# A decoder trunk on one core: the order of all instructions computed in the kernel, instead of by the scheduler that the framework brings

## The chip, the cores and the metric

The kernel runs on 1 core of one Trainium2 chip. The metric is device time in microseconds (us). A core has five engines, each with an instruction queue of its own: TensorE (PE, matmuls and transposes), VectorE (DVE), ScalarE (ACT), GpSimd (POOL) and SyncE (SP, which here only issues transfers). POOL issues the transfers that accumulate into a tile in SBUF. Instructions of different engines are tied by semaphores.

## The reference, cut to what matters

One sequence of 512 tokens, width 1024, goes through two layers, a spatial-gating MLP and a retention, each followed by a dense feed-forward of 2816 hidden columns; all in float32.

```python
def reference(x, positions, mix_norm_g, ...):
    h = x
    for i in range(DEPTH):                       # DEPTH = 2
        hn = rmsnorm(h, mix_norm_g[i])
        if i % N_MIXERS == 0:
            h = h + sgu_mixer(hn, ...)           # gelu(hn @ w_in), u * (W_s LN(v) + b), @ w_out
        else:
            h = h + retention(hn, positions, ...)
        h = h + swiglu(rmsnorm(h, ffn_norm_g[i]), ...)   # (silu(a) * b) @ w_down
    return rmsnorm(h, final_norm_g)

def retention(h, positions, w_in, gn_g, w_out):  # 4 heads, chunks of 128 tokens
    q, k, v, g = jnp.split(h @ w_in, [...], axis=-1)
    q, k = rotary(q, positions), rotary(k, positions) * (RET_QK_DIM ** -0.5)
    scores = jnp.einsum('bhtd,bhsd->bhts', qc, kc) * decay_inner
    ...
    o = o * lax.rsqrt(jnp.mean(o * o, axis=-1, keepdims=True) + EPS)
    return (o.reshape(B, S, RET_V_WIDTH) * gn_g * jax.nn.silu(g)) @ w_out
```

## The kernel before

A float32 product is made of three matmuls on parts: `three` (L246 on) adds high x high, high x low and low x high; L247, L248 and L249 are these three. So each operand is split: ACT makes the high part (L216, `wh_...`), DVE the low part (L223, `wl_...`). The large products use a scheme of seven products in place of eight quarters (`seven`), with the sums of quarters in it named P1, P7, P6, Q4, P5, P2 and P3. A sum of weight blocks is made by DVE, or by an accumulating transfer that POOL issues into a tile already loaded (`add`, L349). A tile that carries P7, P6 and Q4 in turn is named `wr_..._P722`: after DVE has made the low part of one, the next block is added to it.

The residual X lies in SBUF, 4 chunks of 128 tokens by 1024. At a layer's end the last products come by chunk; `norm` sums squares on ACT (L636), `norm_factor` makes the factor (root on ACT L651, the rest on DVE), DVE scales to `xs_...` (L685), and `turn` (L663 on) transposes the chunk with 8 matmuls into a PSUM tile `xT_...`. From it ACT copies the high part `XH_...` (L671), DVE makes `XL_...` (L672), and in layers with `raw_copy` ACT copies it twice more, in halves, into `xr_...` (L704), from which the sums `xP7_...`, `xP5_...`, `xP6_...` of the next scheme are made. PSUM holds four such tiles of 1024 columns; a tile's slot is free when its last reader is done.

The first SGU product (`v0`) starts as chunks of x and weights come in. After the first feed-forward (units gu0_0 to gu0_5, down products dn0_0 and dn0_1) comes the retention: for head 0 the products qk0 and vg0, then rotation with the tables `CS` (sine and cosine, made by `rotary_tables` from positions in exact pieces: 41 DVE instructions of 128x512 in L854 to L895 and two Sin activations). A head ends with scores, values (`pv`), a norm, `sg`, and `turn_z` (L1239 on), which transposes into `zT` and copies to `z` (L1247); the output product `ro` takes the quarters of z and their sums `z_S` (L480) with high (L502) and low part (L506).

What sets the order: the code gives a list of jobs, one per step of matmuls, each with steps of preparation and a lead. `pipeline` runs a job's steps FETCH = 8 jobs ahead for a load, HIGH = 6 for the high part, PREP = 5 for the low part, ADD = 8 for accumulating transfers. Some transposes are put late by hand (`late_one`) or given `high_priority`; a few matmuls are tied behind others by `issue_after`. The rotary tables are cut in pieces by `yield`, and a piece is run after each product of the first feed-forward's unit 2 (`turn_tables`). Then the framework orders the program: the kernel is built with `tile.TileContext(nc, schedule_with_timeline_sim=True)`, which times the instructions on a model and orders each engine's queue by that; tiles are granted in the order in which the code asks for them, from 38 general tiles of 4 KB a partition (`N_GEN`), 5 of 2 KB (`N_TMP`) and the small pools.

Of the kernel before, what the change touches and what calls it, by code (L numbers as in the profile page):

```python
# [32 lines left out]
N_GEN = 38  # L33
N_TMP = 5
# [22 lines left out]
class Job:  # L57
# [3 lines left out]
    def __init__(self, run, steps=(), work=True):  # L61
        self.run, self.steps, self.work = run, list(steps), work


class Chain:
# [26 lines left out]
def pipeline(jobs):  # L92
    weighted = [j for j in jobs if j.steps]
    leads = sorted({n for j in weighted for n, _ in j.steps})
    at = dict.fromkeys(leads, 0)
    done = 0
    for job in jobs:
        for n in leads if done else leads[::-1]:
            while at[n] < min(len(weighted), done + n):
                for m, step in weighted[at[n]].steps:  # L100
                    if m == n:
                        step()
                at[n] += 1
        if job.steps:
            done += 1
        if job.work:
            Chain.all_step()
        job.run()


@with_exitstack
def trunk(ctx, tc, x, positions, mix_g, ffn_g, fin_g, sgu_w_in, sgu_w_s, sgu_b_s, sgu_ln_g, sgu_ln_b,
          sgu_w_out, ret_w_in, ret_gn_g, ret_w_out, ffn_w_gu, ffn_w_down, invf, decay, out):
    nc = tc.nc
    const = ctx.enter_context(tc.tile_pool(name="const", bufs=1))
    xpool = ctx.enter_context(tc.tile_pool(name="xpool", bufs=1))
    gen = ctx.enter_context(tc.tile_pool(name="gen", bufs=N_GEN))
    xp = ctx.enter_context(tc.tile_pool(name="xp", bufs=2))
    tmp = ctx.enter_context(tc.tile_pool(name="tmp", bufs=N_TMP))
    small = ctx.enter_context(tc.tile_pool(name="small", bufs=2))  # L120
    psp = ctx.enter_context(tc.tile_pool(name="psp", bufs=1, space=PSUM))

    W2 = 2 * T
    H = T // 2
# [34 lines left out]
    late = []  # L159
# [3 lines left out]
            late.pop(0)()  # L163

    ident = const.tile([P, P], F32, name="ident")
    make_identity(nc, ident)
# [662 lines left out]
    v = [[None, None] for _ in range(2)]  # L829
# [450 lines left out]
    t = [list(range(4 * hd, 4 * hd + 4)) for hd in range(HEADS)]  # L1280
# [39 lines left out]
```

## Time and profile before

| | us |
|---|---|
| median of 3 runs | 1202.37 (1201.17 to 1203.57) |
| the profiled execution, its own time | 1203.41 |
| its span, first to last instruction | 1201.7 |
| PE busy | 1180.0 |
| DVE busy | 960.9 |
| ACT busy | 664.6 |
| POOL busy | 171.0 |
| mean granted clock of PE | 0.996 |

Busy time is read per engine. A group's row gives line, engine, operation, output and inputs, shape, count, then busy time and mean length in ns, then the idle time of the engine just before, and what ended it. In a timeline row the first number is the start in us, the second the length, and square brackets hold the idle time ahead of it and its releaser. Names in the profile lack their numbers.

### The profile page before, as it was taken

The page shows a single profiled execution, that of the slowest core. Times are in us where ns is not written, and L with a number is a line of the kernel's source. Part 1 is how long each engine was busy: PE and PEld are TensorE (multiplying, and loading weights), DVE is VectorE, ACT ScalarE, POOL GpSimd, SP SyncE. Part 2 cuts the span into 40 slices and gives each one's busy share as a digit, 9 for nine tenths or more (in the row PEclk, how much of TensorE's full clock was granted, in tenths as well). Part 3 has the DMA queues.
Part 4 walks back from the last instruction along what each step waited for, and adds up shares of the span by engine and source line. Part 5 has one row for each costly group of instructions (what it writes and reads, how often), then busy time and mean ns, then how long its engine had stood idle before and what let it go on. Part 6 is the DMA issues. An engine that isn't in the chain of part 4 may idle for free.

```text
span 1201.7 us, 18455 instructions
## 1 busy us (share of the span) xinstructions
PE 1180.0 (98%) x7374; PEld 1067.4 (89%) x7374; DVE 960.9 (80%) x1143; ACT 664.6 (55%) x842; POOL 171.0 (14%) x151
## 2 busy tenths in 40 slices
PE   8999999999999999999999999999999999999997
PEld 7888899989999987988989898878899989999986
DVE  5587998899977789787885959879788896676897
ACT  5523775554444547555664656566565545535465
POOL 1000122121010130110201111220121210101210
PEclk9999999999999999999999999999999999999999
DMA  9912878898684898777677868877868887856892
GB/s 314 282 47 59 244 161 182 226 228 208 160 205 108 225 184 265 176 163 184 155 202 178 192 155 203 183 151 247 217 153 211 186 216 210 199 135 192 168 245 97
DMA packets 128167, 225.90 MB, mean 188 GB/s; under 512 B 7464, under 2 KB 30032, under 8 KB 128080
## 3 DMA queue, kind: packets, MB, share of 16 engines
q1 hardware_dynamic: 88848, 153.37, 38.6%
q0 software_dynamic: 38944, 70.81, 35.3%
q8 instruction: 58, 0.95, 0.3%
q10 hardware_dynamic: 288, 0.52, 0.1%
q14 instruction: 29, 0.24, 0.1%
HBM read 221.53 MB, written 2.10 MB: 186 GB/s over the span
## 4 chain that ended last, share of the span: by engine, by line
PE 85%; DMA 5%; issue 4%; DVE 2%; ACT 2%; POOL 1%; SPq 0%; DVEq 0%; POOLq 0%; ACTq 0%
PE X_gu L247 6%; PE X_gu L249 6%; PE X_gu L248 6%; DMA wr_gu_P<-in_ffn_w_gu 3%; PE Y_gu L249 3%; PE Y_gu L248 3%; PE Y_gu L247 3%; PE X_dn L247 3%; PE X_dn L248 3%; PE X_dn L249 3%; PE X_vg L247 2%; PE X_vg L248 2%; PE X_vg L249 2%; PE ps_v L247 1%; PE Y_dn L248 1%
## 5 line engine op out<-in xcount | busy, mean ns | idle before, releaser
L216 ACT ACTIVATE wh_gu_P<-wr_gu_P 128x1024 fp32r<-128x1024 f32 x132 | 135.3, 1053 | 87.6 <-DVE wr_gu_P L377 51.0
L223 DVE TENSOR_TENSOR wl_gu_P<-wr_gu_P,wh_gu_P 128x1024 fp32r<-128x1024 f32 x132 | 158.7, 1219 | 25.4 <-ACT wh_gu_P L216 25.1
L349 POOL DMA_DIRECT2D wr_gu_P<-in_ffn_w_gu x50 | 60.9, 1258 | 414.0 <-DVE wl_gu_P L223 196.2
L216 ACT ACTIVATE wh_dn_P<-wr_dn_P 128x1024 fp32r<-128x1024 f32 x72 | 69.1, 980 | 42.6 <-DMA wr_dn_P<-in_ffn_w_down 17.8
L223 DVE TENSOR_TENSOR wl_dn_P<-wr_dn_P,wh_dn_P 128x1024 fp32r<-128x1024 f32 x72 | 79.4, 1128 | 2.7 <-issue 1.1
L223 DVE TENSOR_TENSOR wl_vg_P<-wr_vg_P,wh_vg_P 128x1024 fp32r<-128x1024 f32 x48 | 57.8, 1217 | 14.5 <-ACT wh_vg_P L216 14.4
L349 POOL DMA_DIRECT2D wr_dn_P<-in_ffn_w_down x36 | 41.9, 1239 | 143.6 <-DVE wl_dn_P L223 46.6
L216 ACT ACTIVATE wh_vg_P<-wr_vg_P 128x1024 fp32r<-128x1024 f32 x48 | 49.2, 1055 | 22.8 <-DMA wr_vg_P<-in_ret_w_in 16.7
L349 POOL DMA_DIRECT2D wr_vg_P<-in_ret_w_in x26 | 31.5, 1248 | 207.5 <-DMA wr_vg_P<-in_ret_w_in 73.8
L247 PE MATMUL X_gu<-XH_f,wh_gu_P 128*128 128x256 f32 x176 | 50.6, 288 | 2.2 <-ACT xr_f L704 2.2
L247 PE MATMUL Z_gu<-XH_f,wh_gu_P 128*128 128x256 f32 x176 | 50.0, 284 | 1.4 <-DVE s L1051 1.4
L247 PE MATMUL X_gu<-xP5h_f,wh_gu_P 128*128 128x256 f32 x176 | 50.0, 284 | 0.9 <-ACT u L1026 0.9
L249 PE MATMUL Y_gu<-XH_f,wl_gu_Q 128*128 128x256 f32 x176 | 49.9, 284 | 0.8 <-DVE wl_gu_Q L223 0.8
L248 PE MATMUL X_gu<-XL_f,wh_gu_P 128*128 128x256 f32 x176 | 50.5, 287 | 0.0
L249 PE MATMUL X_gu<-XH_f,wl_gu_P 128*128 128x256 f32 x176 | 50.5, 287 | 0.0
L247 PE MATMUL X_gu<-xP6h_f,wh_gu_P 128*128 128x256 f32 x176 | 50.0, 284 | 0.2
L247 PE MATMUL Y_gu<-XH_f,wh_gu_Q 128*128 128x256 f32 x176 | 49.9, 284 | 0.0
L249 PE MATMUL Z_gu<-XH_f,wl_gu_P 128*128 128x256 f32 x176 | 49.9, 283 | 0.0
L248 PE MATMUL X_gu<-xP6l_f,wh_gu_P 128*128 128x256 f32 x176 | 49.8, 283 | 0.0
L249 PE MATMUL X_gu<-xP3h_f,wl_gu_P 128*128 128x256 f32 x176 | 49.8, 283 | 0.0
L248 PE MATMUL X_gu<-xP3l_f,wh_gu_P 128*128 128x256 f32 x176 | 49.8, 283 | 0.0
L249 PE MATMUL X_gu<-xP6h_f,wl_gu_P 128*128 128x256 f32 x176 | 49.8, 283 | 0.0
(643 smaller groups left out, 4284.5 us busy)
## 6 DMA issues: line engine op xcount, KB each, us to landing
wr_gu_P<-in_ffn_w_gu SPq DMA_DIRECT2D x110, 512.0 KB, 5.3
wr_gu_P<-in_ffn_w_gu POOLq DMA_DIRECT2D x50, 512.0 KB, 7.8
wr_dn_P<-in_ffn_w_down SPq DMA_DIRECT2D x50, 512.0 KB, 5.5
wr_vg_P<-in_ret_w_in SPq DMA_DIRECT2D x40, 512.0 KB, 5.8
wr_dn_P<-in_ffn_w_down POOLq DMA_DIRECT2D x30, 512.0 KB, 7.3
wr_vg_P<-in_ret_w_in POOLq DMA_DIRECT2D x26, 512.0 KB, 6.9
wr_ro_P<-in_ret_w_out SPq DMA_DIRECT2D x20, 512.0 KB, 4.8
wr_qk_P<-in_ret_w_in SPq DMA_DIRECT2D x15, 512.0 KB, 5.9
```

The source lines that it names most:

```text
L216: nc.scalar.activation(h, s, AF.Copy)
L223: nc.vector.tensor_tensor(l, s, f32(h), ALU.subtract)
L247: nc.tensor.matmul(o, ah, bh, start=start, stop=False, skip_group_check=True)
L248: nc.tensor.matmul(o, ah, bl, start=False, stop=False, skip_group_check=True)
L249: return nc.tensor.matmul(o, al, bh, start=False, stop=stop, skip_group_check=True)
L349: nc.gpsimd.dma_start(raw[p, 0, g, s][:, 0:nk, :], source(b, g, s, nk), accum_op=ALU.add)
```

## The change

Nothing of the computation, of its tiles' shapes or of the transfers changes. The engines and pools that `trunk` sees are replaced: `rec = Recorder(tc)`, and `nc, tc = rec, rec`. Each call on an engine is recorded as an `Op`, with the tiles and the parts of them that it reads and writes, and the earlier operations on which it depends. The calls to `pipeline` and the jobs now only set in which order operations are recorded; `issue_after` and `high_priority` do nothing. At the end `emit(rec)` computes an order and issues the calls in it, with the framework's own ordering switched off (`manual_schedule`). In the trace of the changed kernel every recorded instruction has the line of the call in `record` (L333).

The order is found in two passes. First, PE's operations in recorded order get the times at which they would run without any wait; `backward` walks from the end and gives each other operation the latest time (`late`) by which it must run for PE. Then a list simulation goes forward: PE takes the earliest recorded operation that can run, each other engine the one with the least `late` (plus three table loads if ACT would have to load another table). SBUF tiles are granted in order of `late`, so that a load is issued as soon as a tile is free for it; PSUM slots follow the recorded order.

```diff
+RESULT = 35
+TO_PE = 55
+HW_DMAS = 8
...
+    if name == "dma_start":
+        kind = "add" if "accum_op" in kwargs else "load" if writes else "store"
+        size = n * 4 * (writes or reads)[0].shape[0]
+        busy = {"SP": 450, "POOL": 1200, "ACT": 100}[engine]
+        took = busy
+        slow = max(60, size * (2 if kind == "add" else 1) * 1350 // 524288)
...
+LAND = 2200
+MARGIN = 600
+TABLE = 1290
...
+def order_of(rec, report=None):
...
+    for op in ops:
+        op.late = None
+        if op.engine == "PE":
+            op.late = at
+            at += op.busy
+    total = at
...
+    backward(ops, lazy, total, gap)
...
+    for key, tiles in classes.items():
+        tiles.sort(key=lambda t: min((o.late, o.n) for o in t.users))
...
+                if e == "PE":
+                    op = min((o for o in queue[e] if can(o)), key=lambda o: o.n, default=None)
+                else:
+                    for o in queue[e]:
+                        if can(o):
+                            if o.kind:
+                                fly = flying["sw" if e == "POOL" else "hw"]
+                                if len(fly) >= HW_DMAS and fly[-HW_DMAS] > now:
+                                    continue
+                            cost = o.late + (3 * TABLE if o.table and o.table != table else 0)
+                            if op is None or (cost, o.n) < best:
+                                op, best = o, (cost, o.n)
...
+    return sorted(ops, key=lambda o: (o.start, o.n))
+
+
+def emit(rec):
+    with rec.tc.manual_schedule():
+        for op in order_of(rec):
+            op.call()
...
-    nc = tc.nc
-    const = ctx.enter_context(tc.tile_pool(name="const", bufs=1))
...
+    rec = Recorder(tc)
+    nc, tc = rec, rec
...
     feed_forward(1, finish)
     pipeline(jobs)
+    emit(rec)
```

Three places of the two orders. In the rows, numbers behind a name are the part, group or step, the last one counts instructions.

At the retention's output, DVE's row before: `X<-X,Y_ro` adds a finished product to the residual, `z_S1_1` and `z_S2_1` are the sums for `z_P6`, of which PE needs the high and low part.

```order
L527 TENSOR_TENSOR X_95<-X_95,Y_ro_7684 128x2x512
L223 TENSOR_TENSOR wl_ro_P6_1_0_7700<-wr_ro_P722_1_0_7431,wh_ro_P6_1_0_7699 128x1024
L480 TENSOR_TENSOR z_S1_1_7749<-z2_1_7009,z3_1_7714 128x1024
L480 TENSOR_TENSOR z_S2_1_7751<-z_S1_1_7749,z2_0_7023 128x1024
L223 TENSOR_TENSOR wl_ro_P6_1_2_7745<-wr_ro_P722_1_2_7457,wh_ro_P6_1_2_7744 128x1024
L506 TENSOR_TENSOR z_P6l_1_7748<-z_S2_1_7751,z_P6h_1_7747 128x1024
```

And DVE's row there in the changed kernel:

```order
L333 TENSOR_TENSOR wl_ro_P6_1_2_7746<-wr_ro_P722_1_2_7502,wh_ro_P6_1_2_7719 128x1024
L333 TENSOR_TENSOR z_S1_1_7755<-z2_1_7039,z3_1_7734 128x1024
L333 TENSOR_TENSOR wl_ro_Q4_0_0_7765<-wr_ro_P722_0_0_7327,wh_ro_Q4_0_0_7751 128x1024
L333 TENSOR_TENSOR z_S2_1_7774<-z_S1_1_7755,z2_0_7069 128x1024
L333 TENSOR_TENSOR z_Q4l_0_7781<-z1_1_6365,z_Q4h_0_7761 128x1024
L333 TENSOR_TENSOR X_82<-X_82,Y_ro_7669 128x2x512
L333 TENSOR_TENSOR z_P6l_1_7802<-z_S2_1_7774,z_P6h_1_7789 128x1024
```

The two sums have moved from behind the residual's addition to ahead of it, and the weights of P6 and the first of Q4 stand ahead of both. On ACT, `z_P6h_1` now follows `wh_ro_Q4_0_0` and `wh_ro_Q4_0_2`, which it preceded; on PE the transposes `zT3_0` stand right behind `zT3_1` and not among the products of P6.

At the start of the second feed-forward, ACT's row before: `XH_f1` and `xr_f1` are copies of the transposed chunks `xT_f1_0` and `xT_f1_1`, `s1_1_0` a copy of a finished product.

```order
L671 ACTIVATE XH_f1_8143<-xT_f1_0_8370 128x8x128
L216 ACTIVATE wh_gu1_1_P1_0_2_8302<-wr_gu1_1_P111_0_2_8229 128x1024
L216 ACTIVATE wh_gu1_1_P2_0_0_8333<-wr_gu1_1_P221_0_0_8237 128x1024
L1026 ACTIVATE s1_1_0_8361<-X_gu1_0_8307 128x1024
L216 ACTIVATE wh_gu1_1_P2_0_2_8364<-wr_gu1_1_P221_0_2_8305 128x1024
L704 ACTIVATE xr_f1_0_0_8381<-xT_f1_0_8370 128x4x128
L671 ACTIVATE XH_f1_8143<-xT_f1_1_8446 128x8x128
L704 ACTIVATE xr_f1_0_1_8382<-xT_f1_0_8370 128x4x128
```

And in the changed kernel:

```order
L333 ACTIVATE XH_f1_8185<-xT_f1_0_8383 128x8x128
L333 ACTIVATE xr_f1_0_0_8408<-xT_f1_0_8383 128x4x128
L333 ACTIVATE xr_f1_0_1_8417<-xT_f1_0_8383 128x4x128
L333 ACTIVATE s1_1_0_8423<-X_gu1_0_8298 128x1024
L333 ACTIVATE wh_gu1_0_P6_0_2_8433<-wr_gu1_0_P722_0_2_8150 128x1024
```

All three readers of `xT_f1_0` now stand side by side.

The rotary tables on DVE, a piece of them before, in the first feed-forward's unit 2 (`s1_0_2`, `y7_0_2` are its gates):

```order
L869 TENSOR_TENSOR turns_2718<-sum11_2936,turn12_2938 128x512
L868 CAST turn14_3003<-turns13_3000 128x512
L1036 SCALAR_TENSOR_TENSOR s1_0_2_2678<-X_gu0_2_2611,s1_0_2_2678 128x512
L223 TENSOR_TENSOR wl_gu0_3_P6_0_0_3059<-wr_gu0_3_P722_0_0_2828,wh_gu0_3_P6_0_0_3058 128x1024
L1036 SCALAR_TENSOR_TENSOR y7_0_2_2749<-y7_0_2_2749,u2_0_2_2820 128x1024
L869 TENSOR_TENSOR frac13_3002<-turns13_3000,turn14_3003 128x512
```

And the last of them in the changed kernel, at the retention's start, where `xP7l_r` and `xP6l_r` are parts that vg0 needs and `ts_q0` is the first use of the tables `CS`:

```order
L333 SCALAR_TENSOR_TENSOR xP7l_r_5119<-xP7_r_5020,xP7h_r_5029 128x1024
L333 TENSOR_TENSOR sum17_5131<-turns_4891,frac16_5110 128x512
L333 TENSOR_TENSOR xP5_r_5138<-xr_r_0_0_4881,xr_r_0_1_4907 128x1024
L333 CAST turn18_5150<-sum17_5131 128x512
L333 TENSOR_TENSOR xP6_r_5154<-xP5_r_5138,xr_r_1_0_4737 128x1024
L333 TENSOR_TENSOR turns_4891<-sum17_5131,turn18_5150 128x512
L333 TENSOR_TENSOR wl_vg0_P6_0_0_5176<-wr_vg0_P722_0_0_4675,wh_vg0_P6_0_0_5069 128x1024
L333 TENSOR_SCALAR quarter_5189<-turns_4891 128x512
L333 TENSOR_TENSOR wl_vg0_P6_0_2_5195<-wr_vg0_P722_0_2_4706,wh_vg0_P6_0_2_5158 128x1024
L333 SCALAR_TENSOR_TENSOR xP6l_r_5202<-xP6_r_5154,xP6h_r_5183 128x1024
L333 CAST turn19_5212<-quarter_5189 128x512
L333 TENSOR_TENSOR ts_q0_5216<-ps_qk0_0_4793,CS_5193 128x1024
```

All 41 have moved from unit 2 to rows 428 to 500 of DVE, up to their first use in row 499. The load of `pos` stands 88 rows later in SP's queue. At the head of SP's queue, where x came first (two pieces of chunk 0, the first weight of v0, six pieces of the other chunks, then the other weights), pieces now alternate: the first weight of v0 and chunk 0 piece by piece, then a weight of v0 and a chunk in turn. ACT has 17 table loads instead of 14. At the tail ACT issues the output's first chunk ahead of the last sum of squares, and not behind it.

More of the change, by code (lines that the diff above doesn't have):

```diff
@@ L108, in pipeline, with __init__, view, __getitem__ @@
         job.run()
+ENGINE_OF = {"tensor": "PE", "vector": "DVE", "scalar": "ACT", "gpsimd": "POOL", "sync": "SP"}
+BANK = 512
+RESULT = 35
+TO_PE = 55
+HW_DMAS = 8
+class Virtual:
+    def __init__(self, rec, pool, shape, dtype, tag, name, bufs, psum):
+        import numpy as np
+        self.rec, self.pool, self.dims, self.dtype, self.tag, self.name, self.bufs = rec, pool, list(shape), dtype, tag, name, bufs
+        free = 1
+        for n in self.dims[1:]:
+            free *= n
+        self.grain = BANK if psum else max(1, free // 64)
+        self.index = np.broadcast_to(np.arange(free).reshape([1] + self.dims[1:]), self.dims)
+        self.users, self.left, self.real, self.history, self.granted = [], 0, None, [], None
+        self.first = None
+    def view(self):
+        return View(self, self.index, ())
+    def __getitem__(self, key):
+        return self.view()[key]
+    def __getattr__(self, name):
+        if name.startswith("_"):
+            raise AttributeError(name)
+        return getattr(View(self, self.index, ()), name)
+    def realize(self):
+        if self.real is None:
+            extra = {} if self.bufs is None else {"bufs": self.bufs}
+            if self.tag is not None:
+                extra["tag"] = self.tag
+            self.real = self.pool.real.tile(self.dims, self.dtype, name=self.name, **extra)
+        return self.real
@@ new lines, with __init__, shape, __getitem__ @@
+class View:
+    def __init__(self, tile, index, path):
+        self.tile, self.index, self.path = tile, index, path
+    @property
+    def shape(self):
+        return list(self.index.shape)
+    def __getitem__(self, key):
+        return View(self.tile, self.index[key], self.path + (("item", key),))
+    def rearrange(self, *a, **k):
+        return View(self.tile, self.index, self.path + (("rearrange", a, k),))
+    def bitcast(self, *a):
+        return View(self.tile, self.index, self.path + (("bitcast", a, {}),))
+    def to_broadcast(self, *a):
+        return View(self.tile, self.index, self.path + (("to_broadcast", a, {}),))
+    def realize(self):
+        t = self.tile.realize()
+        for step in self.path:
+            t = t[step[1]] if step[0] == "item" else getattr(t, step[0])(*step[1], **step[2])
+        return t
+    def mask(self):
+        import numpy as np
+        m = 0
+        for i in np.unique(self.index[0].ravel() // self.tile.grain):
+            m |= 1 << int(i)
+        return m
+    def width(self):
+        n = 1
+        for k in self.index.shape[1:]:
+            n *= k
+        return n
@@ new lines, with __init__, tile, pool @@
+class Pool:
+    def __init__(self, rec, real, bufs, psum):
+        self.rec, self.real, self.bufs, self.psum = rec, real, bufs, psum
+    def tile(self, shape, dtype, tag=None, name=None, bufs=None):
+        return Virtual(self.rec, self, shape, dtype, tag, name, bufs, self.psum)
+class Op:
+    __slots__ = ("n", "engine", "call", "before", "after", "tiles", "new", "busy", "took", "table", "kind", "start", "end",
+                 "late", "left", "ready", "ins", "what", "slow", "then")
+class Recorder:
+    def __init__(self, tc):
+        self.tc, self.real = tc, tc.nc
+        self.ops, self.held = [], {}
+        for attr in ENGINE_OF:
+            setattr(self, attr, EngineProxy(self, attr))
+    def pool(self, real, bufs, psum=False):
+        return Pool(self, real, bufs, psum)
+    def add(self, engine, call, reads, writes, what, busy, took, table=None, kind=None, slow=0):
+        op = Op()
+        op.n, op.engine, op.call, op.what, op.busy, op.took, op.table, op.kind = len(self.ops), engine, call, what, busy, took, table, kind
+        op.before, op.after, op.then, op.tiles, op.new, op.ins, op.slow = set(), [], [], [], [], None, slow
+        seen = set()
+        for views, w in ((reads, False), (writes, True)):
+            for v in views:
+                t, m = v.tile, v.mask()
+                for q, qm, qw in t.history:
+                    if q is not op and (w or qw) and qm & m:
+                        op.before.add(q)
+                if id(t) not in seen:
+                    seen.add(id(t))
+                    op.tiles.append(t)
+                    t.users.append(op)
+                    if t.first is None:
+                        t.first = op
+                        op.new.append(t)
+                        if t.pool.psum:
+                            was = self.held.get(t.tag)
+                            self.held[t.tag] = t
+                            op.before.update(was.users if was else ())
+        for views, w in ((reads, False), (writes, True)):
+            for v in views:
+                t, m = v.tile, v.mask()
+                if w:
+                    t.history = [h for h in t.history if h[1] & ~m]
+                t.history.append((op, m, w))
+        for q in op.before:
+            (q.then if q.engine == engine == "PE" else q.after).append(op)
+        self.ops.append(op)
+        return op
+    def issue_after(self, ins):
+        return nullcontext()
+    def high_priority(self):
+        return nullcontext()
@@ new lines, with backward, post, settle @@
+Recorder.record = record
+LAND = 2200
+MARGIN = 600
+TABLE = 1290
+def backward(ops, lazy, total, gap):
+    import heapq
+    events, serial = [], 0
+    free, pending = {}, {}
+    need, left = {}, {}
+    def post(back, op):
+        nonlocal serial
+        serial += 1
+        heapq.heappush(events, (back, serial, op))
+    def settle(op):
+        for q in op.before:
+            if q.engine != "PE":
+                need[q] = min(need.get(q, total), op.late - gap(op, q))
+                left[q] -= 1
+                if left[q] == 0:
+                    ready(q)
+    def ready(q):
+        place = "dma" if q.kind else q.engine
+        by = need.get(q, total) - (MARGIN if q.kind else q.took - q.busy)
+        pending.setdefault(place, []).append((q, total - by))
+        post(total - by, None)
+    for op in ops:
+        if op.engine != "PE":
+            left[op] = len(op.after)
+    for op in reversed(ops):
+        if op.engine == "PE":
+            post(total - op.late, op)
+        elif not op.after:
+            ready(op)
+    while events:
+        back, _, op = heapq.heappop(events)
+        if op is not None:
+            settle(op)
+        if events and events[0][0] == back:
+            continue
+        for place, queue in pending.items():
+            if free.get(place, back) > back:
+                continue
+            able = [q for q, at in queue if at <= back]
+            if not able:
+                continue
+            q = max(able, key=lambda o: (lazy[o], o.n))
+            queue[:] = [e for e in queue if e[0] is not q]
+            length = q.slow if q.kind else q.busy
+            free[place] = back + length
+            post(free[place], None)
+            q.late = total - back - length - (LAND + q.busy if q.kind else 0)
+            post(total - q.late, q)
```

182 lines of the change are left out of this document (175 added, 7 removed).

## Prediction

> **What bounds the kernel now.** First the busy times of the page, then the table of windows, to see where TensorE (PE) does not run.
>
> ```profile
> span 1201.7 us, 18455 instructions
> ## 1 busy us (share of the span) xinstructions
> PE 1180.0 (98%) x7374; PEld 1067.4 (89%) x7374; DVE 960.9 (80%) x1143; ACT 664.6 (55%) x842; POOL 171.0 (14%) x151
> ```
>
> PE is busy for 98% of the span, and the change takes no matmul away. So all that any other order can win is the time in which PE stands still or runs slowly. The windows say where that lies (columns: window, its length, then busy time of PE, PEld, DVE, ACT and POOL, the granted clock, DMA share, GB/s).
>
> ```profile
> 0.00:20.00 20.00, 16.47 (x71) 13.67 (x72) 10.72 (x16) 12.59 (x19) 3.12 (x12) 1.00 0.91 309
> 20.00:1180.00 1160.00, 1149.46 (x7244) 1042.49 (x7243) 936.49 (x1090) 641.89 (x805) 167.83 (x139) 1.00 0.75 188
> 1180.00:1201.70 21.70, 14.03 (x62) 11.27 (x61) 13.71 (x39) 10.15 (x21) 0.00 (x0) 0.92 0.26 98
> 480.00:500.00 20.00, 20.00 (x140) 18.69 (x139) 18.07 (x28) 13.25 (x23) 1.20 (x1) 1.00 0.74 207
> 500.00:520.00 20.00, 19.00 (x131) 17.23 (x130) 9.80 (x10) 10.59 (x13) 7.33 (x6) 1.00 0.79 139
> 800.00:820.00 20.00, 17.87 (x75) 14.04 (x74) 18.67 (x17) 12.45 (x15) 2.41 (x2) 0.91 0.90 234
> 860.00:880.00 20.00, 17.82 (x126) 16.94 (x125) 15.57 (x25) 12.52 (x18) 2.41 (x2) 0.93 0.60 124
> ```
>
> From 20 to 1180 us PE idles 1160.00 - 1149.46 = 10.5 us. Two windows also show a granted clock under 1: at half clock the share of slow time is twice what is missing, and half of that is lost, so 0.09 x 20 = 1.8 us and 0.07 x 20 = 1.4 us, 3.2 us in all. The middle of the kernel thus holds 13.7 us. The head (3.5 us idle) and the tail (7.7 us) are a matter of first loads and of the last norm. PE's waits, grouped by what ended them, name the causes:
>
> ```profile
> PE xT_in L667 <- DMA X<-in_x: 2.2, 1, 2.2
> PE X_gu L247 <- ACT xr_f L704: 2.2, 1, 2.2
> PE X_ro L247 <- ACT z_P6h L502: 1.6, 1, 1.6
> PE Z_gu L247 <- DVE s L1051: 1.4, 1, 1.4
> ```
>
> Apart from the first load, they are single waits of 1 to 2 us for ACT or DVE, which are busy for 55% and 80%: a matter of order more than of work.
>
> **Place A, the retention output (801 to 809 us).** DVE's timeline before PE's wait for z_P6h:
>
> ```profile
> 801.30 1.22 DVE L527 TENSOR_TENSOR X<-X,Y_ro 128x1024 f32<-128x1024 f32 x1 [2.90 <-PE Y_ro L249]
> 802.44 1.22 DVE L223 TENSOR_TENSOR wl_ro_P<-wr_ro_P,wh_ro_P 128x1024 fp32r<-128x1024 f32 x1
> 803.57 1.22 DVE L480 TENSOR_TENSOR z_S<-z,z 128x1024 f32<-128x1024 f32 x1
> 804.83 1.23 DVE L480 TENSOR_TENSOR z_S<-z_S,z 128x1024 f32<-128x1024 f32 x1
> ```
>
> DVE stood 2.90 us before X<-X,Y_ro until PE closed Y_ro, with the two z_S sums behind it in its queue. The changed order puts both sums ahead of that wait, and PE makes both zT tiles at the start of P7's second half. From there to the first X_ro matmul that needs z_P6, the second half of P7 (24 matmuls) and half of P6 (24) lie in program order. Two neighbours give the cadence:
>
> ```profile
> 800.19 0.39 PE L249 MATMUL Y_ro<-wh_ro_P,z_P7l 128*128 128x512 f32 x1
> 800.42 0.39 PE L247 MATMUL Y_ro<-wh_ro_P,z_P7h 128*128 128x512 f32 x1
> ```
>
> That is 0.23 us, 48 x 0.23 = 11.0 us. The chain is two ACT steps (copy of z, high part; 1.0 us each in ACT's rows of place B, the copy in four pieces somewhat more) and three of DVE (two sums, low part, 1.14 by the starts above): about 6 us, so 5 to spare. A new step stands on this path: z_P6h comes on ACT behind two wh_ro_Q4, whose tiles an accumulating transfer fills; it can eat the 5 us, not more than the rivals allow for below. I count A's 1.6 us as gone.
>
> **Place B, the second feed-forward's start (868 to 877 us).** ACT's timeline before the 2.2 us wait:
>
> ```profile
> 872.31 1.02 ACT L1026 ACTIVATE s<-X_gu 128x1024 f32<-128x1024 f32 x1
> 873.22 1.05 ACT L216 ACTIVATE wh_gu_P<-wr_gu_P 128x1024 fp32r<-128x1024 f32 x1
> 874.16 0.60 ACT L704 ACTIVATE xr_f<-xT_f 128x512 f32<-128x512 f32 x1
> 874.64 1.03 ACT L671 ACTIVATE XH_f<-xT_f 128x1024 fp32r<-128x1024 f32 x1
> 875.54 0.62 ACT L704 ACTIVATE xr_f<-xT_f 128x512 f32<-128x512 f32 x1
> ```
>
> X_gu of unit 1 needs the PSUM slot of xT_f1_0, which the second xr copy frees, at 876.16. By their starts, s and a weight copy (872.31 to 874.16) and the XH_f of the other chunk (874.64 to 875.54) were put before its two parts: 1.85 + 0.90 = 2.75 us, and two weight copies stand before the excerpt. In the changed order the two xr copies follow their XH_f directly, so the slot is free at least 2.75 us earlier and the 2.2 us go. What is late next there is the copies of chunk 1, which free their slot for a tile that comes later.
>
> At s (1.4) and the smaller places the rows of the changed order prepare weights earlier, or take the unit in program order. With the half clock after A and B, all 13.7 us may go. Whether the slow clock goes with the waits is a choice: the only two windows of the middle with a clock under 1 are those with A and B in them, so I take it that the waits bring it.
>
> The Trainium skill, page "TensorE: Matmul & The Clock Gate", section "What's actually happening", says that PE falls to half clock after an idle window of about 3.4 us. Here 1.6 and 2.2 us of waiting stood beside it, so the trace shows less than the page asks; by the page the slow spans would have some other cause, would stay, and the sum would be 3.2 us higher.
>
> **What the change adds.** Place E, the rotary tables: 41 DVE instructions, two Sin activations and the load of pos (88 rows later in SP's queue) leave the first feed-forward's unit 2 and come right before their use, at the retention's start. There DVE also makes XL_r, the xs_r, the sums of xr_r and the weights of vg0. Their durations, by groups:
>
> ```profile
> L869 DVE TENSOR_TENSOR frac<-turns,turn 128x512 f32<-128x512 f32 x5 | 3.4, 682 | 0.0
> ...
> L868 DVE CAST turn<-turns 128x512 int32<-128x512 f32 x5 | 2.2, 435 | 0.0
> ```
>
> In a filled queue each starts about 0.08 us before the one ahead ends (801.30 to 802.44 against 1.22), so I charge 1.14 for 128x1024, 0.60 for a sum of 128x512 and 0.35 for a cast or a scalar product; the 20 sums and 21 small ones of the tables are 12.0 + 7.4 = 19.4 us. From the last XL_r to the tc_q0 that frees ps_qk0 for Z_vg, the changed DVE row has 13 large, 12 middle and 12 small ones: 14.8 + 7.2 + 4.2 = 26.2 us. On PE the same stretch, from the last turn of xT_r (with its copy) to Z_vg, is 108 matmuls of qk0 with half the width (0.12 us each, an estimate from the 0.23) and 72 of vg0: 13 + 16.5, about 29 us. The low half of xP6 comes out at 21.8 against about 23.5 us. The rows ahead of that XL_r, from the last sums of X on, are 15.4 us by the same charges against 14 us of matmuls. So it fits with about a microsecond to spare or to lack: I take 1.0 us of new waits. The lower bound is nothing. The upper one comes from the windows: DVE has 1.9 + 10.2 = 12.1 us free from 480 to 520 us, but most of that is no free room, since it waits there for weights:
>
> ```profile
> 508.24 1.23 DVE L223 TENSOR_TENSOR wl_vg_P<-wr_vg_P,wh_vg_P 128x1024 fp32r<-128x1024 f32 x1 [4.42 <-ACT wh_vg_P L216]
> 513.92 2.36 DVE L223 TENSOR_TENSOR wl_vg_P<-wr_vg_P,wh_vg_P 128x1024 fp32r<-128x1024 f32 x2 [4.46 <-ACT wh_vg_P L216]
> ```
>
> If a fixed order has to sit those 8.9 us out too, 3.2 us are left for 19.4, and 16 us of waits come up. I lean on the row sums, because the changed row has done the weights of qk0 and half of vg0 before this stretch.
>
> Table loads: ACT loads 17 tables instead of 14. Two of the three lie where ACT waits anyway. The third (Sqrt) now stands between the last square and the first root of the norm after the spatial-gating output; before, that table was loaded earlier.
>
> ```profile
> 787.45 1.28 ACT L651 ACT_TABLE_LOAD   x1
> 788.75 0.29 ACT L651 ACTIVATE nf_o<-oss,eps 128x2 f32<-128x2 f32 x1
> ```
>
> That is 1.3 us more in the chain to the first turn of f0, which also stands after 5 matmuls of P3 and not after 12, 7 x 0.23 = 1.6 us earlier in PE's row. Before, PE did not wait for it, with a margin that no row gives: 1.0 us, between 0 and 2.9. The Trainium skill, page "ScalarE: Activation LUTs", section "What ACT_TABLE_LOAD costs", puts a switch at 2.66 us with its drain; the row above shows the next activation 1.30 us after the load began, and by the page this term would be 2.4.
>
> Accumulating transfers: as many as before and released by the same low parts; POOL issues them in almost the same order. Waits of under 1 us for them stay somewhere: 1.0, between 0 and 3.
>
> Head: SP's queue now alternates weights with X.
>
> ```profile
> 0.81 0.85 SPq L795 DMA_DIRECT2D X<-in_x  x2
> 1.72 0.91 SPq L809 DMA_DIRECT2D wr_v<-in_sgu_w_in  x2
> 2.67 3.02 SPq L795 DMA_DIRECT2D X<-in_x  x6
> ```
>
> Before, all of X but chunk 0 followed the first weights; now chunk 0 has two pieces of 256 KB ahead of or between its own and chunks 1 to 3 have one, two and three weights of 512 KB ahead of them. At 309 GB/s (first window) 512 KB are 1.7 us: chunk 0 and 1 come 1.7 us later, chunk 2 3.4, chunk 3 5.1, the weights as much earlier. PE needs both, and has 16 steps of 6 matmuls (1.36 us) to do; it starts later by up to 1.7 us and is fed evenly after that. I take +1.5 us; the bounds are -0.5 (earlier weights win) and +3 (the clock, slow until PE has run for a while, rises one span later).
>
> Tail: on ACT the two issues of the output's chunk 0 now stand ahead of the last square.
>
> ```profile
> 1194.90 0.38 ACTq L787 DMA_DIRECT2D out<-o  x1
> 1195.16 0.61 ACT L636 ACTIVATE sq_dn<-X 128x512 f32<-128x512 f32 x1
> 1195.32 0.46 ACTq L787 DMA_DIRECT2D out<-o  x1
> ```
>
> They cost up to 0.38 + 0.46 us, less what the earlier norms of chunks 2 and 3 win: +0.3, between -0.5 and +1.
>
> **The sum.** The profiled execution took 1203.41 us (span 1201.7 and 1.7 around it), 1.04 above the median of the runs, 1202.37. So 1203.41 - 13.7 + (1.0 + 1.0 + 1.0) + 1.5 + 0.3 = 1194.5, and at the median's scale 1193.5 us. Its own range: with none of the additions, the head at -0.5 and the tail at 0, 1188.2; with E and transfers at 3 and the head at its 3, 1200.0 (2.0 + 2.0 + 1.5 and 1.0 of the rest over the forecast).
>
> **The rivals.**
> *The waits only move* (chance 0.13): a fixed order can stand behind a transfer that lands late, as z_P6h may behind wh_ro_Q4; for it speaks that each queue runs in order. With as much new waiting as old (10.5), but no slow clock, 1203.4 - 13.7 + 10.5 + 1.8 - 1.0 = 1201.0: no measurable change.
> *The slow clock is not brought by these waits* (0.09): then 3.2 us stay, 1196.7. Against it: of the windows of the middle only those two are slow. The Trainium skill's page on TensorE, as told above, speaks for it.
> *The rotary tables fill DVE at the retention's start* (0.10), which ends slower: 16 us of waits there in place of 1.0, and PE then falls to half clock once (1.6, the mean of the two windows): 1193.5 + 15.0 + 1.6 = 1210.1. It decides once all new waits pass 14 us, 13.7 - 1.8 + 2.4. For it speaks that DVE and its wait for weights leave 3.2 us for 19.4, against it the sum of the rows.
> *The order is in effect the old one* (0.02): 1202.4. Against it speak the rows: the tables, the z sums and the xr copies have moved as shown.
>
> **How the numbers follow.** A measurement of this kernel tells about 0.2% from no change, 2.4 us: below 1200.0 is faster, above 1204.8 slower. The forecast has 0.66. Faster: 0.66, 0.09 of the clock rival and 0.02 of the moving waits, 0.77. Same: 0.11 of the moving waits and 0.02 of the last, 0.13. Slower: 0.10. The range goes from 1187 (the lower end, 1188.2, less a microsecond of delays that the windows count as busy, since ends of matmuls are modelled) to 1203, which holds the moving waits and leaves out the rotary rival.
>
> **What would show it.** Idle of PE from 20 to 1180 us near 3 us rather than 10.5; no window there with a clock under 1; no wait of PE for z_P6h or for xr_f before unit 1; Z_vg and xP6 waiting under 2 us in all; a wait of about 1 us at xT_f0; the first ps_v matmul at 10 to 11.5 us. The forecast is wrong if PE's waits name weights or transfers at new places with 10 us together, or if the time from 480 to 520 us holds several us of PE waiting for DVE.

## The result, and the profile after

The changed kernel takes 1265.01 us (median of four runs, 1261.81 to 1267.90) against 1201.77: 1.0523 times as long, with a 95% interval of 1.0495 to 1.0551. The forecast was 1193.5 us, and slower had been given one chance in ten. The profiled execution took 1265.18 us, its span is 61.7 us longer than before. One run of a variant below (both numbers changed) took 1659 us at a granted clock of 0.656 and is left out of the ratios; all others had 0.986 or more. First the busy times of the page:

```profile
span 1263.4 us, 18478 instructions
## 1 busy us (share of the span) xinstructions
PE 1195.9 (95%) x7374; PEld 1071.5 (85%) x7374; DVE 964.8 (76%) x1143; ACT 676.1 (54%) x845; POOL 170.6 (14%) x151
```

The instructions are the same but for the three table loads. ACT is busy 11.5 us longer, of which the loads (1.28 us each) are 3.8 and the rest stays open; PE is busy 15.9 us longer, which is taken apart below. The table of windows, cut at the head and the tail as before:

```profile
0.00:20.00 20.00, 15.60 (x65) 12.80 (x66) 10.19 (x15) 14.16 (x22) 3.13 (x12) 1.00 0.91 329
20.00:1240.00 1220.00, 1166.40 (x7252) 1047.84 (x7251) 941.03 (x1090) 652.67 (x804) 167.50 (x139) 0.99 0.72 178
1240.00:1263.40 23.40, 13.91 (x61) 10.85 (x59) 13.54 (x40) 9.26 (x21) 0.00 (x0) 0.93 0.24 91
```

In the middle PE now idles 1220.00 - 1166.40 = 53.6 us where it idled 10.5. That is 43.1 of the 61.7 us. PE's waits say for whom, and how often (columns: in total, times, longest):

```profile
PE X_gu L333 <- DVE s L333: 10.9, 8, 3.4
PE X_gu L333 <- ACT s L333: 5.5, 2, 3.2
PE pv L333 <- ACT osq L333: 4.8, 6, 0.8
PE sc L333 <- DVE s L333: 3.6, 3, 2.1
PE X_ro L333 <- DVE X L333: 3.4, 2, 2.7
PE ps_u L333 <- DVE ur L333: 3.1, 4, 0.8
PE X_dn L333 <- DVE X L333: 2.8, 2, 2.0
PE ps_v L333 <- ACT v L333: 2.4, 3, 0.8
```

The waits of before (z_P6h, xr_f ahead of a unit, s ahead of Z_gu) are not in the list. In their place stand many short ones, most near 0.8 us, and nearly all of one kind. One of them in PE's timeline, and DVE's at the same time:

```profile
251.07 0.28 PE L333 MATMUL X_gu<-xP3h_f,wl_gu_P 128*128 128x256 f32 x1
251.19 0.28 PE L333 MATMUL X_gu<-xP3h_f,wh_gu_P 128*128 128x256 f32 x1
251.31 0.28 PE L333 MATMUL X_gu<-xP3l_f,wh_gu_P 128*128 128x256 f32 x1
252.37 0.39 PE L333 MATMUL X_gu<-xP3h_f,wl_gu_P 128*128 128x256 f32 x1 [0.78 <-DVE s L333]
252.59 0.28 PE L333 MATMUL X_gu<-xP3h_f,wh_gu_P 128*128 128x256 f32 x1
```

```profile
251.62 0.69 DVE L333 SCALAR_TENSOR_TENSOR s<-X_gu,s 128x512 f32<-128x512 f32 x1 [1.89 <-PE X_gu L333]
252.23 1.22 DVE L333 SCALAR_TENSOR_TENSOR y<-y,u 128x1024 f32<-128x1024 f32 x1
```

The matmul at 251.07 is the last on the first half of the PSUM tile X_gu; the next two already write the second. DVE takes the first half, for the gate's product `s`. It could have begun when the first half was done (251.07 + 0.28 = 251.35), but it begins at 251.62, right behind the end of the second of the other two (251.31 + 0.28 = 251.59; ends of matmuls are modelled). PE stops in the midst of the second half and goes on when DVE is done, though it needs nothing that DVE makes there: its low part wl_gu_P is DVE's work too, but DVE had stood idle for 1.89 us before `s`. PE starts 1.06 us after the matmul before it, where 0.12 is usual: a wait of 0.78 costs 0.94.

Over PE's whole timeline (waits over 0.25 us, after the first 20 us) 43 waits of 43.7 us have matmuls on the same PSUM tile, by its name, on both sides, and 42 of these end with an instruction that reads this tile; 6 of 10.6 us lie between two tiles. Before, there were 6 of each kind, with 5.3 and 5.0 us, and only 1 of the 6 within a tile ended with a reader of it: the other 5 were for an operand. The clock records of the trace show half clock for 23.9 us ahead of the tail, before for 6.8 (the last stretch, at the span's end, is 5.6 us and was 5.7).

So the 61.7 us are 43.1 of idle time in the middle, 1.7 by which the window of the tail is longer, and 1166.40 - 1149.46 = 16.9 of more busy time in the middle. Of these 16.9, the slow clock is (23.9 - 6.8) / 2 = 8.5, the interruptions about 5.9 (37 more waits at the 0.16 of the one above, an estimate), and work that the head left over 16.47 - 15.60 = 0.9; 1.6 stay open.

### The profile page after: what moved, and what is told of

Same layout as the page of the kernel before. It is cut to its first block, busy times and chain, and to the rows that moved or that the text cites. A ratio compares the mean times of both kernels' runs of the same rounds, so it can differ in the third digit from the quotient of the medians.

```text
span 1263.4 us, 18478 instructions
## 1 busy us (share of the span) xinstructions
PE 1195.9 (95%) x7374; PEld 1071.5 (85%) x7374; DVE 964.8 (76%) x1143; ACT 676.1 (54%) x845; POOL 170.6 (14%) x151
## 5 line engine op out<-in xcount | busy, mean ns | idle before, releaser
L333 DVE TENSOR_TENSOR wl_gu_P<-wr_gu_P,wh_gu_P 128x1024 fp32r<-128x1024 f32 x132 | 158.7, 1220 | 54.2 <-ACT wh_gu_P L333 34.9
L333 ACT ACTIVATE wh_gu_P<-wr_gu_P 128x1024 fp32r<-128x1024 f32 x132 | 135.8, 1054 | 103.5 <-DMA wr_gu_P<-in_ffn_w_gu 44.1
L333 POOL DMA_DIRECT2D wr_gu_P<-in_ffn_w_gu x50 | 60.9, 1272 | 399.1 <-DVE wl_gu_P L333 170.5
L333 ACT ACTIVATE wh_dn_P<-wr_dn_P 128x1024 fp32r<-128x1024 f32 (+1 forms) x72 | 69.5, 983 | 66.4 <-PE X_gu L333 25.0
L333 DVE TENSOR_TENSOR wl_dn_P<-wr_dn_P,wh_dn_P 128x1024 fp32r<-128x1024 f32 (+1 forms) x72 | 80.5, 1131 | 15.2 <-PE X_gu L333 5.3
L333 POOL DMA_DIRECT2D wr_dn_P<-in_ffn_w_down x36 | 41.8, 1208 | 185.4 <-DMA wr_dn_P<-in_ffn_w_down 93.9
L333 DVE TENSOR_TENSOR wl_vg_P<-wr_vg_P,wh_vg_P 128x1024 fp32r<-128x1024 f32 x48 | 57.5, 1219 | 9.0 <-ACT wh_vg_P L333 7.9
L333 POOL DMA_DIRECT2D wr_vg_P<-in_ret_w_in x26 | 31.6, 1243 | 203.2 <-DVE wl_vg_P L333 71.4
L333 PE MATMUL X_gu<-xP3l_f,wh_gu_P 128*128 128x256 f32 x176 | 51.4, 292 | 7.0 <-DVE s L333 7.0
L333 ACT ACTIVATE wh_vg_P<-wr_vg_P 128x1024 fp32r<-128x1024 f32 x48 | 48.8, 1060 | 16.5 <-DMA wr_vg_P<-in_ret_w_in 11.6
L333 PE MATMUL X_gu<-xP6h_f,wh_gu_P 128*128 128x256 f32 x176 | 51.5, 292 | 5.5 <-ACT s L333 5.5
L333 PE MATMUL X_gu<-xP3h_f,wl_gu_P 128*128 128x256 f32 x176 | 51.8, 294 | 4.7 <-DVE s L333 3.9
L333 PE MATMUL X_gu<-xP3h_f,wh_gu_P 128*128 128x256 f32 x176 | 51.1, 290 | 0.8 <-DVE he L333 0.8
L333 PE MATMUL X_gu<-xP5h_f,wh_gu_P 128*128 128x256 f32 x176 | 49.9, 284 | 1.7 <-ACT u L333 1.7
L333 PE MATMUL X_gu<-xP6l_f,wh_gu_P 128*128 128x256 f32 x176 | 51.0, 290 | 0.0
L333 PE MATMUL X_gu<-xP6h_f,wl_gu_P 128*128 128x256 f32 x176 | 51.0, 290 | 0.0
L333 PE MATMUL Y_gu<-xP7h_f,wh_gu_P 128*128 128x256 f32 x176 | 50.5, 287 | 0.0
L333 PE MATMUL Y_gu<-xP7l_f,wh_gu_P 128*128 128x256 f32 x176 | 50.4, 286 | 0.0
L333 PE MATMUL Y_gu<-xP7h_f,wl_gu_P 128*128 128x256 f32 x176 | 50.3, 286 | 0.0
L333 PE MATMUL X_gu<-XH_f,wh_gu_P 128*128 128x256 f32 x176 | 50.0, 284 | 0.0
L333 PE MATMUL Z_gu<-XH_f,wh_gu_P 128*128 128x256 f32 x176 | 49.9, 284 | 0.0
L333 PE MATMUL Z_gu<-XL_f,wh_gu_P 128*128 128x256 f32 x176 | 49.9, 284 | 0.0
```

Of the source, the lines that this page charges most:

```text
L333: return fn(*[real_of(a) for a in args], **{k: real_of(a) for k, a in kwargs.items()})
```

## Experiments

Theory 1: an instruction that touches one half of a PSUM tile waits for those issued ahead of it, on other engines, that touch the other half. The planner keeps the halves apart (BANK = 512 elements, a tile has 1024) and so plans no wait. Theory 2: DVE and ACT run late behind transfers, wherever the halves stand. What theory 1 asks of PE's order can be read from the two orders with their waits. Before, at the end of unit 2 (rows shortened to the places where the tile changes):

```
X_gu0_2 <- xP3h_f0, wl_gu0_2_P3_0_2       last matmul of the first half
X_gu0_3 <- XH_f0, wh_gu0_3_P1_0_0         48 matmuls of the next unit's P1, and one of its P7
X_gu0_2 <- xP3h_f0, wh_gu0_2_P3_0_0       first matmul of the second half [waits DVE]
```

In the old order 49 other matmuls stand in front of the wait on DVE. In the changed order the second half follows the first directly.

**The planner told of whole tiles.** One number:

```diff
-BANK = 512
+BANK = 1024
```

> One number of the planner is changed: parts of a PSUM tile are told apart by 1024 elements (the whole tile) and not by 512 (its halves). Theory 1 (an instruction that touches one half of a PSUM tile waits for all issued ahead of it on other engines that touch the other half; the planner does not know it): the 43 waits of 43.7 us in which the matmuls before and after write the same PSUM tile go nearly all, and with five of them the half clock behind them, about 8 us; 1265 - 52 = 1213 us, 1205 to 1222. Theory 2 (ACT and DVE run late behind transfers, wherever the halves stand): waits stay at the same places, 1255 to 1270 us.

Measured 1225.79 us, 1.0198 times before (1.0182 to 1.0214). The waits within a tile fall from 43 to 4, from 43.7 to 3.5 us, and only one of the four ends with a reader of the tile: theory 1 holds, and theory 2 alone is out. But the time is 4 us over theory 1's range and 13 us over what I expected, since the waits between tiles grew from 10.6 to 20.2 us, and half clock is still 23.9 us. The largest of them:

```profile
PE X_gu L333 <- ACT s L333: 6.0, 2, 3.4
PE xT_f L333 <- DVE xs_f L333: 4.1, 3, 2.2
PE X_gu L333 <- ACT u L333: 3.8, 1, 3.8
```

ACT's timeline ahead of the first of the two waits for s (2.6 us, PE goes on at 295.6):

```profile
287.84 1.04 ACT L333 ACTIVATE wh_gu_P<-wr_gu_P 128x1024 fp32r<-128x1024 f32 x1
293.59 1.06 ACT L333 ACTIVATE wh_gu_Q<-wr_gu_P 128x1024 fp32r<-128x1024 f32 x1 [4.71 <-DMA wr_gu_P<-in_ffn_w_gu]
294.55 1.00 ACT L333 ACTIVATE s<-X_gu 128x1024 f32<-128x1024 f32 x1
```

The copy s, which frees X_gu for P6, stands behind a weight whose accumulating transfer was issued at 283.62 and landed at 293.50, 9.9 us later. By its constants the planner counts 1.2 + 2.2 + 2.7 = 6.1 us for it if no other transfer is ahead, where the median of POOL's 50 transfers into wr_gu is 7.7 us in this run (7.8 before), and 4.0 for a load, where the median of the 110 into wr_gu is 5.1. That is theory 3: a second cause.

**The same order, readers issued later.** The computed order stays, but each ACT or DVE instruction on a PSUM tile goes behind the matmuls on it that followed, up to the first instruction that needs its result:

```diff
+def readers_later(ops):
+    at = {op: i for i, op in enumerate(ops)}
...
+            end = min([at[q] for q in op.after + op.then], default=len(ops))
...
+            late = [at[q] for t in op.tiles if t.pool.psum for q in t.users if q.engine == "PE" and i < at[q] < end]
+            if late:
+                place[op] = (max(late), 1, i)
...
-        for op in order_of(rec):
+        for op in readers_later(order_of(rec)):
```

> The order is that of the changed kernel, but each ACT or DVE instruction that uses a PSUM tile is issued behind the matmuls on that tile that stood next behind it, as far as nothing that needs it comes. Theory 1 (order of issue makes the wait): PE no longer waits between the halves, the readers come one to three us later; the same-tile waits fall from 43.7 us to under 10, other waits grow by some us; 1215 to 1235 us. Theory 2 (late queues): nothing is won, since the readers come later still; 1262 to 1275 us.

Measured 1241.81 us, 1.0328 (1.0300 to 1.0356): 23 us won by making readers later. The waits within a tile halve only, to 21 of 21.0 us, where I expected under 10 (I take it that the limit often comes before the half's end, but did not count it); those between tiles grow to 15.4. The time is 7 us over theory 1's range: the direction is theory 1's, the size I had too large.

**No reader of a half.** In the feed-forward units the gate's product is made once, when both halves are done:

```diff
                 elif p == "P3" and n == 4:
-                    product(1, acc["X"], st_["s1"], slice(2 * c, 2 * c + 2))
+                    if c == 1:
+                        product(1, acc["X"], st_["s1"], slice(0, 4))
```

> In the feed-forward units the gate's product is made once, on the whole tile, when P3 is done, in place of one for each half. Theory 1: the ten waits between the halves of P3 in these units (2.9, 3.4 and eight of 0.78 us, 12.5 us in all) go, with the half clock behind the two long ones (1.7 and 3.4 us lost), less some waits for the later product: 1265 - 14 = 1251, 1246 to 1257 us. Theory 2: the product comes 1.4 us later and nothing is won, 1264 to 1270 us.

Measured 1254.12 us, 1.0430 (1.0405 to 1.0455), within the range of theory 1. Waits within a tile go from 43 to 35 and fall by 11.2 us; the half clock stays at 23.9 us, against the expectation, and waits between tiles grow to 13.5.

**The old kernel without foreign matmuls between the halves.** The reverse: in the kernel before, the products of units 2, 3, 5 and 4 and of the down projections are tied behind the last matmul of the product before.

```diff
+                if i == 0 and name[:2] in ("gu", "dn") and not tied:
+                    acc["end"] = xn["last"]
                 for c in range(2):
                     with tc.issue_after(xn["turned"].ins) if (p, n) in tied and c == 0 else nullcontext():
-                        matmuls(p, g, s, nk, c)
+                        with tc.issue_after(acc["end"].ins) if "end" in acc and c == 0 else nullcontext():
+                            matmuls(p, g, s, nk, c)
```

> The kernel before, with the matmuls of P1 to Q4 of units 2, 3, 5 and 4 and of the down products tied behind the last matmul of the product before, so that the scheduler can't put them between the two halves of P3 as it does in eight units. Theory 1: eight waits of 0.8 us or more come up between the halves, some longer where DVE's queue is full, and perhaps half clock behind them: 1202 + 7 to 14, 1209 to 1216 us. Theory 2: nothing but a few shifts, 1201 to 1205 us.

Measured 1215.10 us, 1.0113 (1.0092 to 1.0134). PE's waits show the eight, by name:

```profile
PE X_gu L247 <- DVE s L1040: 6.9, 6, 1.7
...
PE X_gu L247 <- DVE he L1040: 1.6, 2, 0.8
```

The old scheduler and the old code give the same wait at the same place once nothing may be put there. Half clock is 10.2 us here, 3.4 more than before, but one stretch of 3.4 lies in the head, ahead of all eight; from 20 us on it is 6.8, as before.

**Transfers counted as slower.** Theory 3 by itself and with theory 1:

```diff
-BANK = 512
+BANK = 1024
-LAND = 2200
+LAND = 4000
```

> The planner with whole PSUM tiles (1024) and a transfer that it counts as landing 1.8 us later (LAND 4000 in place of 2200: 5.8 us for a load of 512 KB and 7.9 for an accumulating one, near the 5.3 and 7.7 us that the runs show, where it had 4.0 and 6.1). Theory 3 (of what is left with whole tiles, the larger part is ACT standing in a weight's high part whose transfer lands later than planned, with a copy that PE needs behind it: 3.8 + 2.6 + 1.8 + 3.4 + 1.1 us, and half clock behind each, about 8 us): most of it goes, 1226 - 16 = 1210, 1203 to 1217 us. Rival (a fixed order as such: real times scatter, and waits come up at other places): 1219 to 1230 us.

> The changed kernel with its planner's halves left (512) and only the landing 1.8 us later (LAND 4000). Theory 1 and 3 together (two causes side by side): the six waits between different tiles, 10.6 us, shrink by half or more with some half clock behind them, the 43 waits within a tile stay: 1265 - 10 = 1255, 1247 to 1260 us. If late transfers were the main cause, it would come under 1235 us.

Both numbers: 1203.45 us, 1.0013 times before (1.0000 to 1.0026), 7 us better than I expected. LAND alone: 1248.41 us, 1.0388 (1.0371 to 1.0406). What each does, in us of the profiled executions (waits as number and sum after the first 20 us, half clock ahead of the tail):

| kernel | time, median | waits within a tile | between tiles | half clock |
|---|---|---|---|---|
| before | 1201.5 to 1202.9 | 6, 5.3 | 6, 5.0 | 6.8 |
| changed | 1265.0 | 43, 43.7 | 6, 10.6 | 23.9 |
| whole tiles | 1225.8 | 4, 3.5 | 11, 20.2 | 23.9 |
| LAND 4000 | 1248.4 | 50, 42.4 | 2, 2.6 | 6.8 |
| both | 1203.5 | 2, 2.4 | 6, 5.5 | 3.4 |

Of the waits within a tile, those that end with a reader of this tile are 1, 42, 1, 48 and 0 in the five rows. So whole tiles take away the waits for readers of the other half, and the later landing most of those between tiles. The two causes also meet. In the changed kernel 13.7 of the 23.9 us of half clock come with three waits within a tile, those that end at 221.6, 877.2 and 960.4 us. Around the first of them ACT, DVE and PE show:

```profile
217.53 1.06 ACT L333 ACTIVATE wh_gu_Q<-wr_gu_P 128x1024 fp32r<-128x1024 f32 x1 [4.26 <-DMA wr_gu_P<-in_ffn_w_gu]
218.62 1.23 DVE L333 TENSOR_TENSOR wl_gu_Q<-wr_gu_P,wh_gu_Q 128x1024 fp32r<-128x1024 f32 x1 [2.30 <-ACT wh_gu_Q L333]
220.89 0.69 DVE L333 SCALAR_TENSOR_TENSOR s<-X_gu,s 128x512 f32<-128x512 f32 x1
221.63 0.39 PE L333 MATMUL X_gu<-xP3l_f,wh_gu_P 128*128 128x256 f32 x1 [2.86 <-DVE s L333]
```

A transfer lands late, so DVE's wl_gu_Q comes late, with the gate's product behind it in DVE's queue, and the wait between the halves becomes 2.86 us in place of 0.78. With LAND alone the longest wait for this product is 1.1 us and the half clock falls to 6.8, while the waits within a tile stay. What is left with both, by PE's waits:

```profile
PE Z_dn L333 <- DVE h_P2l L333: 1.8, 1, 1.8
PE xT_f L333 <- DVE xs_f L333: 1.7, 4, 0.7
PE X_ro L333 <- DVE X L333: 1.6, 1, 1.6
PE Z_dn L333 <- ACT h_P2h L333: 1.1, 1, 1.1
```

**Still more room for transfers.** Three further values, with whole tiles: LAND 6000; LAND 4000 and 1.5 us more for accumulating transfers alone; LAND 4800.

> As before, but with 3.8 us more (LAND 6000: 7.8 and 9.9 us, about where nine of ten transfers have landed). Theory 3: the rest of those waits goes too, 1200 to 1212 us, at or under the run with 4000. Rival (too much room for transfers pushes other work late): over the run with 4000, 1215 to 1230 us.

> Whole PSUM tiles and LAND 4000, and accumulating transfers alone counted as landing 1.5 us later still (9.4 us). Of the waits left with LAND 4000 (7.9 us in the middle), those of s_dn (0.9), u (0.6) and of the last down product (1.1 and 1.8, with half clock behind, 1.7) have a high part of an accumulated weight ahead on ACT. Theory 3: they go for the most part, 1203 - 4 = 1199, 1197 to 1202 us, which would be faster than both kernels. Rival (from here on each change of the planner's numbers only deals the waits anew): 1201 to 1209 us.

> Whole PSUM tiles and LAND 4800 for all transfers, between the two runs with 4000 and 6000. If the time falls and rises smoothly with this number, it lies between 1203 and 1206 us; if each value deals the waits anew, anywhere from 1200 to 1212 us.

Measured 1208.04 (1.0051, 1.0036 to 1.0066), 1206.82 (1.0039, 1.0024 to 1.0054) and 1214.22 us (1.0091, 1.0072 to 1.0109), with 13.7, 10.2 and 13.7 us of half clock. None beats the old kernel, and 4800 between 4000 and 6000 is the slowest of the four, over both ranges that I gave for it. At 4800 single waits come up at new places:

```profile
PE X_so L333 <- DVE X L333: 3.6, 1, 3.6
PE X_gu L333 <- ACT xr_f L333: 2.9, 1, 2.9
PE Z_dn L333 <- DVE wl_dn_P L333: 2.6, 2, 1.8
```

Room for transfers beyond 4000 wins nothing: 6000 lies in the range that I gave for theory 3, but over the run with 4000 and not under it, and my 1199 us for the second is missed. That each value near the real durations deals a few long waits anew is the reading that fits, but the runs don't show why 4800 is worse than 6000. No version faster than both kernels was found.

## Why the prediction was wrong

*What can be won* (13.7 us in the middle): right in kind. The old waits for z_P6h, for xr_f ahead of a unit and for s ahead of Z_gu are gone in the changed kernel, and with whole tiles and LAND 4000 none of them comes back.

*What the change adds* (3.0 us): the step that failed, and the half of it that was missing is larger than all that I summed. The sum has a term for the rotary tables, one for the table load and one for the accumulating transfers, and none for a wait of PE on a PSUM tile that it is still filling: it was put at nothing without a reason. I looked at what moved on DVE, ACT and SP, and at PE's row only around the transposes `zT` and those of f0. What the sum left out are the matmuls that the old order has between the two halves of a PSUM tile and the changed one has not. Without them there are 43 waits of 43.7 us, and about 6 us more for the interruptions (the estimate above). That is shown three ways: by telling the planner (39 us come back, 1265.0 to 1225.8), by removing the reader of a half (11 us), and by forcing the halves together in the old kernel (8 waits, 13 us). Along PE's timeline the output tile, by its name, changes 246 times where it changed 378 times before, and 301 times with whole tiles; that difference was the thing to explain. That the order of issue makes these waits is shown; whether the chip needs them or only the framework puts them into the program is not, since no run leaves the order and takes the wait out.

*Accumulating transfers* (1.0 us, between 0 and 3): the mechanism was named, as the risk at z_P6h and in the rival of moving waits, and the size was wrong. The waits between tiles are 10.6 us in the changed kernel, where they were 5.0, and 20.2 once the waits within tiles are gone. LAND alone brings them down to 2.6, the half clock to 6.8, and takes 16.6 us off. I had the planner's own constants in the diff and the landing times of 7 to 8 us on the page, and did not set one beside the other.

*The slow clock*: that the waits bring it was right, as the last section shows. I counted on none being left in the middle; it grew from 6.8 to 23.9 us. The Trainium skill, page "TensorE: Matmul & The Clock Gate", section "What's actually happening", puts half clock behind an idle window of about 3.4 us. The profiles here show that less idle time is enough: the wait of 2.86 us that ends at 221.6 us is followed by 3.4 us of half clock, and the last section has the count.

*Rotary tables* (1.0 us, and the rival that ends slower): about right in size. No wait for xP6 or for Z_vg's slot comes up in the changed kernel, and one of 1.4 us for k0h, the rotated keys, ahead of the scores; with whole tiles and LAND 4000 no wait over 0.3 us stands at the retention's start. The sum of the rows was the right view, the free time in the windows not: the kernel is slower, but not by this rival's mechanism.

*Table load ahead of f0's first turn* (1.0 us): with whole tiles and LAND 4000 PE waits 0.8 us there for xs_f; that the load is the cause was not tried. *Head* (+1.5): PE's busy time in the first 20 us is 15.60 against 16.47, +0.9; the first ps_v matmul starts at 9.1 us, before the 10 to 11.5 that I named. *Tail* (+0.3): from the 62nd matmul before the end it takes 24.0 us where it took 21.9, +2.1, of which 0.9 is a wait within the tile X_dn.

*The rivals*: "The waits only move" was given 0.13 and at most as much new waiting as old; it was the nearest. New waits were five times the old (54.3 us against 10.3), because the planner does not only move them: it is blind to a dependence that the program enforces. Of the two signs that I named for a wrong forecast, neither is what came: PE's new waits name mostly readers of its own PSUM tile, not weights or transfers, and from 480 to 520 us PE waits 2.0 us for DVE, once.

## What to carry to other kernels

A planner that computes an order must know every dependence that the program will enforce, at the grain at which it is enforced: read the waits of the built program, not the code's intent. When an order changes, ask first what the rows were for that disappear from between two steps on the engine that bounds the kernel. Set the planner's constants beside the measured durations, above all for transfers, since an engine that runs in order stands still behind one that lands late, with everything queued behind it.

## What the runs showed of the hardware

How long PE may wait before its clock falls can be read over the eleven profiles. Of the waits with no other within 7 us, outside the first and the last 20 us, none of 93 from 0.6 to 1.8 us was followed by half clock, 5 of 11 from 1.8 to 2.3 us, and 18 of 20 over 2.3 us. Half clock ahead of the tail lasts 3.4 us, or a multiple. So a wait of 2.5 us that brings one such stretch costs 2.5 + 3.4 / 2 = 4.2 us, an estimate.

Where the wait lies decides too. In each profile the starts of half clock are whole multiples of 3.413 us apart (in the changed kernel 25, 167, 24, 26 and 46 of them), so the time can be cut into stretches of this length. Of the stretches at full clock, outside the first and the last 20 us, all 29 in which PE stood idle for 1.95 us or more in sum were followed by half clock, 5 of 17 with 1.5 to 1.95 us, and none of 180 with 0.5 to 1.5 us. With LAND 4800 a wait of 2.94 us, up to 162.9 us, fell on two stretches, 1.7 us on one and 1.2 on the next, and brought none.
